# Matrix products emitted in steps of four row tiles or two column tiles beside the chains of two recurrent layers

## The chip, the cores and the metric

The kernel runs on one core of a Trainium2 chip. The metric is the device time of one execution in microseconds (us), lower is better. Five engines work side by side, each on its own queue of instructions and each in the order of its queue: TensorE (PE in the profile, its weight loads PEld), VectorE (DVE), ScalarE (ACT), GpSimd (POOL) and SyncE (SP, which issues most of the DMAs).

## The reference, cut to what matters

The model is one attention block with expert retrieval, followed by two layers of a recurrent network of width 1024 over 528 positions (16 learned tokens and 512 of the input). Only the two recurrent mixers are touched by the change:

```python
def gated_deltanet(h, w_in, w_conv, a_log, dt_bias, w_norm, w_out):
    qkv, z, beta_pre, a_pre = jnp.split(h @ w_in, ...)
    qkv = causal_conv_silu(qkv, w_conv)
    ...
    o = chunk_gated_delta_rule(q, k, v, g, beta)   # a triangular solve and a scan over chunks
    o = rms_norm(o, w_norm) * jax.nn.silu(z)
    return o @ w_out

def mlstm(h, w_in, gate_bias, w_norm, w_out):
    q, k, v, o, gates = jnp.split(h @ w_in, ...)
    ...                                            # a scan over chunks
    return (rms-normed scan output * sigmoid(o)) @ w_out
```

Each mixer is thus a large product in (`h @ w_in`), a recurrence over chunks of positions that is a long chain of small dependent products, and a large product out.

## The kernel before, in words

All tensors lie with the features on the 128 partitions and the positions along the free axis; a large product takes one tile of 128 output features at a time ("column tile") and runs over the 8 tiles of 128 input features ("row tiles"). To keep float32 accuracy each operand is split in a high and a low part, so one row tile is three matmuls for each half of the 528 positions: six matmuls of 264 columns (lines 71, 72 and 76 in `mm_segs`). A column tile of the products in is 8 row tiles, so 48 matmuls; a column tile of the product out of one pair of heads is 2 row tiles, so 12 matmuls. Both accumulate in one of two PSUM tiles of two banks each (`Acc`); VectorE empties them (lines 1544 and 1558 for the products in, line 1605 for the product out).

The gated delta net (`gdn_block`) works on eight pairs of heads, q = 0 to 7, one pass for each. Two chains run over the passes. The preparing chain (`prepare`, then `tokens`) builds the inverse of each chunk's triangular matrix: norms (line 1633), the products `kk` and `kq` (1673, 1674), a long VectorE stretch that ends in `ex` (1691), the product `rep` (1697), another VectorE stretch, and then three levels, each of transposes `xt` (1734), products `py` (1740) and products `pz` (1752). `tokens` turns k and v (1769, 1777). The scanning chain (`scan`) runs over six chunks: the state times k and q (`pks` 1798, `pqs` 1803), VectorE's `rr` (1801), `pv` (1810), ScalarE's `vr` (1812), `psu` and `po` (1817, 1831), VectorE's new state `S` (1823) and output `ot` (1836), which is then normed on ScalarE and GpSimd (1839 to 1843). A third one (`normed`) turns the finished outputs (`ofm`, 1863) and splits them into `oh` and `ol` (1866, 1868), on which the product out works.

What stands where in the program is set by a planner, `Weave.run`: the chains and the stream of large products (`products2`) are Python generators. A chain yields the TensorE time of what it has just emitted and the time after which its next piece is due; whenever a chain is due it is emitted, and otherwise the stream of products is advanced to its next `yield`, which says what that step cost. `gemm_steps` yields after every two row tiles (12 matmuls, 1.3 us in the planner's account), `out_part` after every column tile (12 matmuls, 1.35 us). The planner's clock is a plan and not a measured time. A unit of products may be emitted once its `ready` test holds: q and k of a pass when the scan two passes back is done, v when the tokens of the pass before are turned, z and the product out when `normed` has delivered. In all, the products in of this layer are 48 column tiles and the products out 64.

The compiler of the kernel language then takes the emitted order as a priority and places an instruction that is emitted later ahead of one that it expects to be still waiting. The order on TensorE's queue is fixed after that.

`mlstm_block` does the same for four pairs of heads, with `interleave` in the place of the planner: it advances the products or the chain (`core`), whichever has done the smaller share of its total. Its products in go through `gemm_steps` as well (23 column tiles); its product out (`unit_out`) has a loop of its own.

Of the kernel before, what the change touches and what calls it, by code (L numbers as in the profile page):

```python
# [17 lines left out]

P = 128
D = 1024  # L20
KT = 8
S = 512
NM = 16
# [41 lines left out]
def mm_segs(nc, x, items, start, stop):  # L65

    xh, xl = x
    for s in range(len(items[0][0])):
        sl = items[0][0][s][1]
        for segs, (lh, ll) in items:  # L70
            nc.tensor.matmul(segs[s][0], lh, xh[:, sl], start=start, stop=False)  # L71
            nc.tensor.matmul(segs[s][0], ll, xh[:, sl], start=False, stop=False)  # L72
    for s in range(len(items[0][0])):
        sl = items[0][0][s][1]
        for segs, (lh, _) in items:
            nc.tensor.matmul(segs[s][0], lh, xl[:, sl], start=False, stop=stop)  # L76


def setup(tc, es, A):
# [27 lines left out]
    g.queue = []  # L107
    g.h = [None] * KT
    h_tiles(g)
# [3 lines left out]
def h_tiles(g):  # L113
    for k in range(KT):
        g.h[k] = g.res.tile([P, T], F32, tag=f"h{k}", name=f"h{k}")
# [44 lines left out]
def wpre(g, name, *idx):  # L160

    key = (name, idx)
    if key not in g.pre:
        wstart(g, name, *idx)
        g.pre[key] = wload(g, g.raw.pop(key), g.wp, 3)


def wget(g, name, *idx):

    key = (name, *idx)  # L170
    wpre(g, *key)
    if key in g.queue[:1]:
        g.queue.pop(0)
        for k in g.queue[:2]:
            wpre(g, *k)
        for k in g.queue[2:3 if g.third is None else 4]:
            wstart(g, *k)
    return g.pre.pop((name, idx))


def gemm_fm(g, segs, name, ct, rhs):


    run_steps(gemm_steps(g, segs, name, ct, rhs, lambda: None))
# [66 lines left out]
def rsqrt_rows(g, segs, n):  # L251

    rs = g.np_.tile([P, T], F32, tag="rs", name="rs", bufs=1)
    for p, sl in segs:
        g.nc.scalar.activation(rs[:, sl], p, AF.Sqrt, bias=g.eps, scale=1.0 / D)
    g.nc.vector.reciprocal(rs[:, 0:n], rs[:, 0:n])
# [46 lines left out]
def xn_tiles(g):  # L303
    xh = [g.res.tile([P, T], F32R, tag=f"xh{k}", name=f"xh{k}") for k in range(KT)]
    xl = [g.res.tile([P, T], F32R, tag=f"xl{k}", name=f"xl{k}") for k in range(KT)]
    return xh, xl
# [152 lines left out]
def gemm_steps(g, segs, name, ct, rhs, out):  # L459

    npc, _, nk, _ = g.A[name][ct].shape
    for pc in range(npc):
        hi, lo = wget(g, name, ct, pc)
        for k in range(nk):
            mm_segs(g.nc, rhs(pc * nk + k), [(segs, (hi[:, k], lo[:, k]))], pc == 0 and k == 0, pc == npc - 1 and k == nk - 1)
            if k % 2:
                yield 1.3
    out()


# [107 lines left out]
def attention_block(g, tail):  # L578

    tc, nc, A = g.tc, g.nc, g.A  # L580
    with ExitStack() as es:
# [12 lines left out]
        ni = NormIn(g, "norm1", NM, S, lambda tag: sp.tile([P, 512], F32, tag="sb", name=tag, bufs=6) if tag == "xt" else gp.tile([P, 512], F32, tag="gate0", name=tag))  # L594
        for k in range(KT):
            nc.sync.dma_start(g.h[k][:, NM:], A["xT"][k])
            if k < 2:
                wpre(g, "w_in", 0, k)
        for k in range(KT):
            ni.step(k)  # L600
# [364 lines left out]
class Rows:  # L965


    def __init__(self, g, es):
        self.g = g
        nc = g.nc  # L970
        self.p = es.enter_context(g.tc.tile_pool(name="p_rows", bufs=1))
        self.x = self.p.tile([P, D], F32, name="rx")
        self.o = self.p.tile([P, D], F32, name="ro")
        self.hid = self.p.tile([P, NJ], F32, name="rhid")
# [38 lines left out]
    def step(self):  # L1013

        nc = self.g.nc
        while self.nf < min(self.n + UG, 2 * NJ):
            e, j = divmod(self.nf, NJ)
            t = self.p.tile([P, D], F32, tag="row", name="row", bufs=UG)
            nc.gpsimd.indirect_dma_start(out=t, out_offset=None, in_=(self.U, self.V)[e],  # L1019
# [371 lines left out]
def v2(t):  # L1391
    return t.rearrange("p (s n) -> p s n", s=2)
# [5 lines left out]
class GdnNorm:  # L1398
# [30 lines left out]
    def rows(self, ps, ms1):  # L1429
# [6 lines left out]
        nc.gpsimd.memset(ms1[:, 0:NM], 1.0)  # L1436
        nc.vector.tensor_scalar(ms1[:, NM:], p1, 1.0 / D, EPS, op0=ALU.mult, op1=ALU.add)
        rs = self.g.np_.tile([P, T], F32, tag="rs", name="rs", bufs=1)
        for p, sl in zip(p2, SEG2):
            nc.vector.scalar_tensor_tensor(rs[:, sl], ms1[:, sl], EPS * D, p, op0=ALU.mult, op1=ALU.add)  # L1440
        nc.scalar.activation(rs, rs, AF.Sqrt, scale=1.0 / D)
# [18 lines left out]
def gdn_block(g, ni, tail):  # L1460
    tc, nc, A = g.tc, g.nc, g.A
    with ExitStack() as es:
# [72 lines left out]
        def fm(ct, out):  # L1535
            segs, ps = acc.get()
            return gemm_steps(g, segs, "gdn_in", ct, ni.X, lambda: out(ps))
# [60 lines left out]
        def out_part(q, c4):  # L1598
            hi, lo = wget(g, "gdn_out", q, c4)
            for i in range(4):  # L1600
                ct = 4 * c4 + i
                segs, ps = acc.get()
                for k in range(2):
                    mm_segs(nc, done["og", q][k], [(segs, (hi[:, 2 * i + k], lo[:, 2 * i + k]))], k == 0, k == 1)
                nc.vector.tensor_tensor(v2(g.h[ct]), v2(g.h[ct]), ps, op=ALU.add)
                if q == 7:
                    tail.step(ct)
                yield 1.35
            clk.put(("out", q, c4))

        def units_out(q):
            return [([("gdn_out", q, c4)], lambda: clk.ready(("og", q)), lambda c4=c4: out_part(q, c4)) for c4 in range(2)]
# [358 lines left out]
def mlstm_block(g, ni, tail):  # L1971

    tc, nc, A = g.tc, g.nc, g.A
    with ExitStack() as es:
# [70 lines left out]
        def unit(ct, ready, out, n=T):  # L2045
            def fn():
                segs, ps = acc.get(n)
                if n == S:
                    segs = [(ps, slice(NM, T))]
                return gemm_steps(g, segs, "mlstm_in", ct, ni.X, lambda: out(ps))  # L2050
            return [("mlstm_in", ct, 0)], ready, fn
# [224 lines left out]
```

## Time and profile before

| | |
|---|---|
| median of 3 timed runs | 3642.78 us (3641.7 to 3643.01) |
| the profiled execution, its own time | 3628.02 us |
| its span, first to last instruction | 3626.3 us |
| TensorE busy | 3483.1 us, 96% of the span |
| gated delta net, about 1940 to 2640 us | TensorE busy 675.08 of 700 us, granted clock 0.95 |
| mLSTM, about 3015 to 3265 us | TensorE busy 237.97 of 250 us, granted clock 0.99 |

The profile is of one execution. A matmul's record shows how long it was in the array, and records overlap; the pitch from one start to the next tells the rate. One float32 matmul of the chains shows as two records. "Idle before" is the time in which the engine did nothing just before an instruction, and the arrow names what ended it.

### The profile page before, as it was taken

What the parts mean: (1) busy time and instruction counts of PE and PEld (TensorE: products, weight loads), DVE (VectorE), ACT (ScalarE), POOL (GpSimd) and SP (SyncE); (2) the same over time, 40 slices, a digit from 0 to 9 for tenths busy, and PEclk for the clock granted to TensorE, in tenths of its full rate; (3) what the DMA queues carried; (4) which work ended last, traced back from release to release, by engine and by line L of the source; (5) the groups of instructions that cost most, each with busy time, mean ns of one, the idle gap of its engine ahead of it and who ended that gap; (6) DMA issues with size and microseconds to landing.
All of it is one profiled execution on the core that took longest, in us unless ns stands there. A gap on an engine that the chain in (4) does not pass through costs nothing. (4 is left out here: it accounts for less than half of the span.)

```text
span 3626.3 us, 56462 instructions
## 1 busy us (share of the span) xinstructions
PE 3483.1 (96%) x21979; PEld 3164.9 (87%) x21979; DVE 2399.4 (66%) x4395; ACT 1591.4 (44%) x2998; POOL 776.2 (21%) x828
## 2 busy tenths in 40 slices
PE   8999999999898889999999999999999999999999
PEld 6777888898887779999998899999899998878887
DVE  5764457999967658888887677767643345564433
ACT  4555333333477763333346444445422235343222
POOL 2421010333322232333332322222100003120000
PEclk9999999999999999999998999999999999999999
DMA  4233233566678889999972121111132322213222
GB/s 134 76 88 88 82 124 122 198 225 221 233 237 279 270 299 369 358 360 353 363 257 77 56 63 57 47 52 52 48 98 90 94 88 83 75 59 99 93 93 93
DMA packets 169492, 557.60 MB, mean 154 GB/s; under 512 B 19617, under 2 KB 20130, under 8 KB 169224
## 3 DMA queue, kind: packets, MB, share of 16 engines
q1 hardware_dynamic: 90228, 313.50, 26.1%
q0 software_dynamic: 49136, 170.64, 14.2%
q10 hardware_dynamic: 29860, 69.84, 5.3%
q8 instruction: 173, 2.83, 0.3%
q14 instruction: 95, 0.78, 0.1%
HBM read 492.20 MB, written 55.41 MB: 151 GB/s over the span
## 5 line engine op out<-in xcount | busy, mean ns | idle before, releaser
L72 PE MATMUL ps<-xh,wlo 128*128 128x264 f32 (+2 forms) x3296 | 1051.3, 331 | 45.0 <-DVE wlo L149 44.8
L71 PE MATMUL ps<-xh,whi 128*128 128x264 f32 (+2 forms) x3296 | 1069.6, 337 | 18.8 <-ACT xh L288 13.5
L149 DVE TENSOR_TENSOR wlo<-raw,whi 128x1024 fp32r<-128x1024 f32 x562 | 718.6, 1279 | 531.2 <-ACT whi L147 524.8
L147 ACT ACTIVATE whi<-raw 128x1024 fp32r<-128x1024 f32 x562 | 594.5, 1058 | 978.9 <-PE ps L76 782.6
L76 PE MATMUL ps<-xl,whi 128*128 128x264 f32 (+2 forms) x3296 | 813.1, 331 | 6.5 <-DVE xl L289 6.4
L72 PEld LDWEIGHTS ps<-xh,wlo 128*128 128x128 f32 x3296 | 629.6, 192 | 91.5 <-DVE wlo L149 61.4
L71 PEld LDWEIGHTS ps<-xh,whi 128*128 128x128 f32 x3296 | 630.2, 192 | 59.3 <-ACT xh L288 15.9
L76 PEld LDWEIGHTS ps<-xl,whi 128*128 128x128 f32 x3296 | 563.6, 192 | 39.3 <-DVE xl L289 8.9
L1019 POOL DMA_INDIRECT row<-in_peer_ur_dram,rix x128 | 146.1, 1142 | 465.7 <-DVE row L1028 372.1
L71 PE MATMUL ps<-ah,whi 128*128 128x264 f32 (+1 forms) x768 | 230.1, 320 | 0.0
L72 PE MATMUL ps<-ah,wlo 128*128 128x264 f32 (+1 forms) x768 | 229.9, 320 | 0.0
L55 PE MATMUL ps<-ah,whi 128*128 128x384 f32 x640 | 215.5, 337 | 0.0
L56 PE MATMUL ps<-ah,wlo 128*128 128x384 f32 x640 | 215.1, 336 | 0.0
L1019 POOL DMA_INDIRECT row<-in_peer_v_dram,rix x128 | 138.1, 1079 | 276.9 <-DVE ro L1032 261.5
L280 POOL TENSOR_TENSOR ssum<-ssum,sq 128x512 f32<-128x512 f32 (+1 forms) x49 | 75.1, 1538 | 460.4 <-ACT sq L279 459.8
L1028 DVE SCALAR_TENSOR_TENSOR row<-row,rx 128x1024 f32<-128x1024 f32 x128 | 164.0, 1283 | 6.2 <-DMA row<-in_peer_ur_dram,rix 6.2
L1333 ACT ACTIVATE ah<-gt 128x384 fp32r<-128x384 f32 x128 | 67.3, 526 | 227.4 <-DVE gt L1331 227.4
L76 PE MATMUL ps<-al,whi 128*128 128x264 f32 (+1 forms) x768 | 163.2, 321 | 0.0
L1214 ACT ACTIVATE hot<-hot,lt 128x128 f32<-128x128 f32 x384 | 122.0, 390 | 93.3 <-DVE hot L1212 89.6
L1032 DVE SCALAR_TENSOR_TENSOR ro<-row,rhid,ro 128x1024 f32<-128x1024 f32 x127 | 162.4, 1278 | 0.6 <-DMA row<-in_peer_v_dram,rix 0.4
L71 PEld LDWEIGHTS ps<-ah,whi 128*128 128x128 f32 x768 | 144.3, 188 | 11.4
L72 PEld LDWEIGHTS ps<-ah,wlo 128*128 128x128 f32 x768 | 144.3, 188 | 10.9
(429 smaller groups left out, 6184.7 us busy)
## 6 DMA issues: line engine op xcount, KB each, us to landing
raw<-in_peer_u_dram SPq DMA_DIRECT2D x128, 512.0 KB, 5.5
raw<-in_peer_v_dram SPq DMA_DIRECT2D x128, 512.0 KB, 6.9
raw<-in_ff_up_dram SPq DMA_DIRECT2D x64, 512.0 KB, 3.4
raw<-in_ff_down_dram SPq DMA_DIRECT2D x64, 512.0 KB, 3.5
at<-Ad POOLq DMA_DIRECT2D x32, 768.0 KB, 7.2
raw<-in_gdn_in_dram SPq DMA_DIRECT2D x48, 512.0 KB, 3.5
Gd<-G ACTq DMA_DIRECT2D x62, 384.0 KB, 3.2
gt<-Gd ACTq DMA_DIRECT2D x62, 384.0 KB, 5.2
```

Of the source, the lines that this page charges most:

```text
L55: nc.tensor.matmul(out, lh, rh, start=start, stop=False)
L56: nc.tensor.matmul(out, ll, rh, start=False, stop=False)
L71: nc.tensor.matmul(segs[s][0], lh, xh[:, sl], start=start, stop=False)
L72: nc.tensor.matmul(segs[s][0], ll, xh[:, sl], start=False, stop=False)
L76: nc.tensor.matmul(segs[s][0], lh, xl[:, sl], start=False, stop=stop)
L147: nc.scalar.activation(hi, raw, AF.Copy)
L149: nc.vector.tensor_tensor(lo, raw, r32(hi), op=ALU.subtract)
L280: g.nc.gpsimd.tensor_tensor(self.t[:, 0:n], self.t[:, 0:n], sq[:, 0:n], op=ALU.add)
L1019: nc.gpsimd.indirect_dma_start(out=t, out_offset=None, in_=(self.U, self.V)[e], in_offset=bass.IndirectOffsetOnAxis(ap=self.ix[:, j:j + 1] ...
L1028: o = nc.vector.scalar_tensor_tensor(t, t, 1.0, self.x, op0=ALU.mult, op1=ALU.mult, accum_out=a)
L1032: o = nc.vector.scalar_tensor_tensor(self.o, t, a, self.o, op0=ALU.mult, op1=ALU.add)
L1214: nc.scalar.activation(oh[:, j], o2[:, j], AF.Copy, scale=lt[:, 2, 4 * t4 + j:4 * t4 + j + 1])
```

## The change

`gemm_steps` yields after every four row tiles (24 matmuls) instead of two, with 2.6 us for the step instead of 1.3; `out_part` yields after every second column tile, with 2.7 us instead of 1.35 for one. What is computed, the number of instructions, the tiles and the buffers stay the same.

```diff
+STEP = 4
@@ gemm_steps
             mm_segs(g.nc, rhs(pc * nk + k), [(segs, (hi[:, k], lo[:, k]))], pc == 0 and k == 0, pc == npc - 1 and k == nk - 1)
-            if k % 2:
-                yield 1.3
+            if k % STEP == STEP - 1:
+                yield 0.65 * STEP
@@ out_part
                 if q == 7:
                     tail.step(ct)
-                yield 1.35
+                if i % 2:
+                    yield 2.7
             clk.put(("out", q, c4))
```

## Rows read from the trace of the kernel before

**Rows 1.** The page: span, and each engine's busy time, share and instructions.
```profile
span 3626.3 us, 56462 instructions
PE 3483.1 (96%) x21979; PEld 3164.9 (87%) x21979; DVE 2399.4 (66%) x4395; ACT 1591.4 (44%) x2998; POOL 776.2 (21%) x828
```

**Rows 2.** Busy time by stretch: both layers, and the last scan.
```profile
core 0: us, PE busy (x) PEld busy (x) DVE busy (x) ACT busy (x) POOL busy (x), PEclk, DMA share, GB/s
1940.00:2640.00 700.00, 675.08 (x5849) 639.84 (x5848) 505.26 (x1222) 343.31 (x798) 178.77 (x226) 0.95 0.19 58
3015.00:3265.00 250.00, 237.97 (x1596) 200.94 (x1595) 152.54 (x306) 120.86 (x304) 51.51 (x73) 0.99 0.22 72
2573.60:2605.60 32.00, 31.99 (x255) 31.18 (x256) 16.10 (x33) 15.05 (x48) 5.32 (x12) 1.00 0.20 65
```

**Rows 3.** Waits of TensorE, 1940 to 2640 us: total us, times, longest.
```profile
PE rep L1697 <- DVE ex L1691: 10.0, 8, 2.9
PE ps L71 <- DVE h L1605: 4.9, 4, 1.6
```

**Rows 4.** Timeline of TensorE: start, us, instruction xcount, idle before: rep of two passes.
```profile
2204.30 1.72 PE L1697 MATMUL rep<-ex,nblk 88*88 88x450 f32 x4 [0.82 <-DVE ex L1691]
2279.34 0.96 PE L1697 MATMUL rep<-ex,nblk 88*88 88x450 f32 x2 [0.82 <-DVE ex L1691]
```

**Rows 5.** The same view, a step of products between two scan pieces, q = 7.
```profile
2582.88 0.60 PE L1831 MATMUL po<-vr,dt 88*88 88x128 f32 x4
2583.24 0.37 PE L71 MATMUL ps<-oh,whi 128*128 128x264 f32 x1
2583.44 0.28 PE L72 MATMUL ps<-oh,wlo 128*128 128x264 f32 x1
2583.57 0.28 PE L71 MATMUL ps<-oh,whi 128*128 128x264 f32 x1
```

**Rows 6.** The same view: first products beside that scan, its last piece, and ofm.
```profile
2570.09 0.47 PE L71 MATMUL ps<-oh,whi 128*128 128x264 f32 x1
...
2602.21 0.60 PE L1831 MATMUL po<-vr,dt 88*88 88x128 f32 x4
...
2605.57 1.07 PE L1863 MATMUL ofm<-c_ident,ot 88*128 88x88 f32 x12
```

**Rows 7.** Timelines of TensorE, DVE and ACT: the scan's links in its last chunks.
```profile
2595.58 0.61 PE L1817 MATMUL psu<-vr,kd 88*128 88x128 f32 x4
2596.23 0.61 DVE L1823 SCALAR_TENSOR_TENSOR S<-S,lastb,psu 128x128 f32<-128x128 f32 x2 [3.65 <-PE psu L1817]
2598.78 0.60 DVE L1801 SCALAR_TENSOR_TENSOR rr<-pks,na,vs 88x128 f32<-88x128 f32 x2
2600.28 0.60 PE L1810 MATMUL pv<-rr,Z 88*88 88x128 f32 x4
2600.92 0.38 ACT L1812 ACTIVATE vr<-pv 88x256 f32<-88x256 f32 x1
2605.35 0.69 ACT L1843 ACTIVATE ot<-ot,ss 88x128 f32<-88x128 f32 x2 [1.08 <-POOL ss L1841]
```

**Rows 8.** Busy time in a level stretch, and TensorE's timeline there.
```profile
2226.73:2236.97 10.24, 10.24 (x84) 9.49 (x83) 4.23 (x10) 5.71 (x12) 7.01 (x7) 0.50 0.17 41
2226.37 0.41 PE L1734 MATMUL xt<-c_ident,Z 44*44 44x44 f32 x6
2226.71 0.59 PE L71 MATMUL ps<-xh,whi 128*128 128x264 f32 x1
...
2234.97 0.42 PE L71 MATMUL ps<-xh,whi 128*128 128x264 f32 x1
2235.19 0.42 PE L72 MATMUL ps<-xh,wlo 128*128 128x264 f32 x1
```

**Rows 9.** Waits of TensorE in the mLSTM layer, 3010 to 3270 us.
```profile
PE inter L2170 <- ACT nd L2171: 2.9, 2, 1.7
```

## The prediction

> **What bounds the kernel now.** I read the page first. TensorE is busy 96% of the span and no other engine over 66% [rows 1], so a reordering can gain only what TensorE loses in the two layers that it touches. The busy times by stretch give that loss: in the gated delta net TensorE is busy 675.08 of 700 us, so 24.9 us are idle; in the mLSTM 237.97 of 250, so 12.0 us are idle [rows 2]. The change alters no instruction and no count, so the rest of its effect can only come from where TensorE's instructions stand: idle time, the price of going from a chain's piece to a product and back, and the granted clock, 0.95 in the first layer against 0.99 in the second [rows 2].
>
> The list of waits says which idle time there is: the first entry is `rep`, which waits 10.0 us in eight passes for VectorE's `ex` [rows 3], most passes 0.82 us [rows 4]; the next, 4.9 us, is the last product out waiting for its PSUM tiles [rows 3], after all chains have ended, where the emission has no freedom and the change none either. The passes follow each other at 2279.34 - 2204.30 = 75.0 us [rows 4], with almost no other idle time: TensorE's work sets the period, the chains do not.
>
> The timeline then shows how the steps lie. Beside the last scan they lie as emitted: a piece of the scan, twelve products, the next piece [rows 5]; this begins at 2570.09 and ends with the last piece at 2602.21 [rows 6], and over these 32 us TensorE is busy 31.99 us [rows 2]. In the level stretch it is otherwise: single products, cut out of their step, stand between the transposes [rows 8]. So the emitted order is kept where everything is ready, and where a chain is late the compiler fills the hole with whatever product is free, whatever the step size.
>
> **The change, part by part.**
>
> (a) *Fewer crossings.* The first product after a scan piece takes 2583.44 - 2583.24 = 0.20 us to the next start, the following ones about 0.12 (2583.57 - 2583.44 = 0.13) [rows 5]: a crossing costs 0.08 us. The gated delta net has 48 x 4 + 64 = 256 steps before and 128 after, so at most 128 x 0.08 = 10.2 us are saved, and nothing where the compiler mixes the two streams anyway [rows 8]. Both patterns are in the trace; I take half, -5.1. In the mLSTM 23 x 4 = 92 steps become 46: at most 3.7, taken -1.8.
>
> (b) *`rep` later in the queue.* Between the last `kq` and `rep` the planner now puts products in pieces of 2.6 instead of 1.3, so `rep` stands about one short step later, and VectorE has more time for `ex`. That is more than the 0.82 us that are missing [rows 4], if the step really lies there; where the products have run out by then, nothing changes. Bounds 0 and 8 x 0.8 = 6.4 us; I take about half, -3.
>
> (c) *The pool of the last pass.* While the scan of q = 7 runs, there are only 8 column tiles of the product out and 2 of z left, 8 + 2 x 4 = 16 short steps. Today they cover the 15 links of chunks 1 to 5 one for one (the last gets two). Now they are 8 long steps, each of which stands behind one link: they are used up after `pv` of the third chunk, and what follows has no cover. The links bare: `vr` ends at 2600.92 + 0.38 = 2601.30, 0.42 us after `pv` (2600.28 + 0.60); `S` ends at 2596.84, 0.65 us after `psu` (2595.58 + 0.61), of which `po`, which follows `psu`, covers 0.4; `rr` takes 0.60 us, of which `pqs` covers 0.4 [rows 7]. Together 0.42 + 0.25 + 0.2 = 0.87 us a chunk, and two chunks 1.7. After the last `po`, which ends at 2602.81 [rows 6], `ot` is normed until 2605.35 + 0.69 = 2606.04 [rows 7]: 3.2 us, covered now by the last two steps, then bare. Sum 4.9 us; up to 1.4 comes back, since ScalarE has the eviction of z out of the way earlier. I take +4.
>
> (d) *Levels and tokens of the last pass.* The same happens once before: v of q = 7 and z of q = 6 are 16 short steps beside twelve pieces of `prepare` and `tokens`; as 8 long ones they run out during the levels. I count four to six bare pieces at 0.42 to 0.87 us: 2 to 5, taken +3; below, 0, if scan pieces of q = 6 fall there.
>
> (e) *The clock.* In a level stretch of the steady passes TensorE is busy all of 10.24 us and its clock is 0.50 (1.2 of 2.4 GHz); before the fall it did transposes and small products with single large products between them, before the rise a run of large products [rows 8]. A product then takes 2235.19 - 2234.97 = 0.22 us, against 0.12 [rows 5, 8]. Some 24 products in such a stretch lose 24 x 0.10 = 2.4 us, and the transposes about 1: 3.5 us, an estimate. Bare pieces, as in (c) and (d), look more like that stretch than like the rest; none to two further stretches, 0 to 7 us, taken +2.
>
> (f) *mLSTM core.* With half as many steps, a core piece more often follows a core piece; the longest such wait today is 1.7 us and all are 2.9 [rows 9]. Products of the next pair are free to fill in. 0 to 6, taken +2.
>
> (g) *Chains behind longer steps.* VectorE's additions and evictions keep their number; a chain's piece stands on average 0.5 x 12 x 0.12 = 0.7 us later on TensorE's queue. In passes 1 to 6 I cost this at nothing: TensorE's other work hides it, as the period is work and not chain [rows 4]. If that cover is gone, it is the slower rival below.
>
> The sum: -5.1 - 1.8 - 3 + 4 + 3 + 2 + 2 = +1.1 us on the profiled execution's 3628.02, so 3629.1; that execution is 14.8 us under the median of the timed runs, and with the same distance the median goes from 3642.78 to about 3644.
>
> **The rivals.**
>
> *The covers run out in every pass (slower).* The products of a pass are gated: q and k of the next pass wait for a scan to end, v for the tokens. Long steps use up what is open early in a pass, behind links that need 0.2 to 0.9 us [rows 7], and the later links and the levels stand bare. Then each of six passes pays two or three chunks at 0.87 plus one more half-clock stretch of 3.5 us, as in (c) and (e): 2.5 to 6 us, together 15 to 36, less the 10 of (a) and (b), plus the 11 of (c) to (f): 3659 to 3680. It decides once more than about 1 us per pass can't be filled. For it: the product-poor level stretch exists today [rows 8]. Against it: the fill-in seen there, and PSUM has room for two column tiles (96 products, about 11.7 us) to be drawn forward.
>
> *The gains in full (faster).* (a) and (b) at their ends, -10.2 - 3.7 - 6.4, with only (c) to pay: -16, 3627. For it: the regular alternation of [rows 5], where each crossing would be saved. Against it: the broken steps of [rows 8].
>
> *The clock stays up (faster).* Runs of products twice as long could keep the clock at its upper level through the levels. The mean of 0.95 over 700 us [rows 2] is about 700 x 0.05 / 0.5 = 70 us at 0.50, as much as seven stretches of 10.24 us; at 3.5 us each, -24, so 3619. Against it: what stands between the levels today is single products that the compiler placed, and a step's size does not change what is ready there.
> The Trainium skill speaks for this rival: "TensorE: Matmul & The Clock Gate", section "Loop structure matters more than you think", says that the loop structure decides whether matmuls stay warm, and asks for matmuls kept back to back. The trace agrees that the long runs have the full clock, but shows the clock low in a stretch in which TensorE is never idle [rows 8].
>
> *The change hardly reaches the queue (no change).* Emission is a priority only; if the compiler's placing evens it out, the time is 3643 within 3 us. For it: [rows 8]. Against it: [rows 5, 6], where the steps lie as emitted.
>
> **How the numbers follow.** My forecast, gains and losses about even, has 0.32 and lies between 3636 and 3652; no change at all 0.13; the covers run out in every pass 0.30; the gains in full 0.16; the clock stays up 0.09. Bounds 0.2% either way (7.3 us, about what a measurement of this kernel can tell from no change): 3635.5 to 3650.1. The two middle cases lie inside, 0.45 with nearly all of their range; slower is the first rival, 0.30; faster the two others, 0.25. The predicted time is the forecast's, 3644. The range for 8 in 10 goes from 3626, just past the gains in full, to 3668, the middle of the slower rival; about 0.09 is left out below and 0.1 above.
>
> **What would show it.** After the change: steps of 24 beside the last scan, eight of them, then pieces of the scan with no product between them from the third chunk's `psu` on, and TensorE idle for some 3 us before `ofm`. The entry of `rep` among the waits falls from 10.0 towards 4, or (b) is wrong. The distance from `rep` to `rep` in the steady passes stays at 75.0 us or falls by about 1; if it grows by 2 or more, the slower rival holds, and the idle time or the half-clock stretches in that pass say which half of it. The busy-time rows of the mLSTM stay within 3 us. The forecast is wrong if the gated delta net's stretch changes by more than 7 us either way.

## The result and the profile after

The change makes the kernel slower: the median goes from 3642.78 us (7 runs in this comparison, 3629.42 to 3646.69) to 3658.5 us (7 runs, 3654.81 to 3670.54), a ratio of 1.0053 (95% interval [1.0033, 1.0073]). The same kernel run again in another set (`e7_change_again` below) gave 3658.33 us and again 1.0053 [1.0034, 1.0073]. The forecast was 3644, about even, and is 14.5 us short. The time lies above the 3650.1 up to which the prediction spoke of no change, so the sign is that of the first rival. The range of 3626 to 3668 held it because it reached to the middle of that rival, not because the sum was right.

One thing has to be known before the traces are compared. The profiled execution of after took 3670.54 us and is the longest of its seven, that of before took 3628.02 us and is shorter than any of its seven here, so the spans below differ by 42.5 us where the medians differ by some 16. The second run's profiled execution (3651.04 us, span 3649.2 us) has the same order and is used beside it. It is the shortest of its ten, as that of before is shorter than its seven, so these two compare better: their spans differ by 22.9 us.

The page of after: span, and TensorE's busy time, share and instructions ([rows 1] of before).

```profile
span 3668.8 us, 56447 instructions
PE 3511.0 (96%) x21979; PEld 3189.5 (87%) x21979; DVE 2393.3 (65%) x4395; ACT 1602.7 (44%) x3003; POOL 770.7 (21%) x828
```

Busy time by stretch in after: the gated delta net, the mLSTM (35 us later than in before), the two parts of a level stretch of the fourth pass, q = 3 (columns as in [rows 2]).

```profile
1940.00:2640.00 700.00, 666.78 (x5635) 630.22 (x5633) 470.24 (x1186) 338.53 (x781) 165.23 (x219) 0.92 0.18 55
3050.00:3300.00 250.00, 236.60 (x1567) 199.93 (x1567) 143.99 (x297) 118.55 (x297) 46.39 (x70) 0.96 0.22 70
...
2228.50:2231.40 2.90, 0.41 (x5) 0.25 (x3) 1.33 (x2) 0.98 (x4) 1.94 (x2) 1.00 0.28 34
2231.40:2262.00 30.60, 30.56 (x229) 28.52 (x230) 11.12 (x27) 11.56 (x33) 7.71 (x9) 0.56 0.14 45
```

In the first layer TensorE now is idle 33.2 of 700 us, against 24.9 in [rows 2], and its clock is 0.92 instead of 0.95. In the mLSTM 13.4 us are idle instead of 12.0. The list of waits names what is new. TensorE in after, 1900 to 2700 us: total us, times, longest ([rows 3]).

```profile
PE rep L1700 <- DVE ex L1694: 7.8, 8, 2.3
PE xt L1737 <- ACT xe L1738: 6.2, 3, 2.5
...
PE psu L1820 <- ACT vr L1815: 4.2, 5, 2.3
PE ps L73 <- DVE h L1607: 3.3, 2, 2.2
PE ps L73 <- DVE xs L1546: 2.3, 2, 1.7
...
PE ofm L1866 <- ACT ot L1846: 1.8, 1, 1.8
```

`rep` has fallen from 10.0 to 7.8 us, as step (b) wanted. But an entry that was not there stands second: a transpose of the levels, `xt`, waits 6.2 us for ScalarE's copy `xe`, twice for 2.5 us and once for 1.1. It is to be found in the two passes that were steady before. In the timeline `rep` of these passes now stands as follows ([rows 4]; the next one begins at 2386.69).

```profile
2215.89 1.75 PE L1700 MATMUL rep<-ex,nblk 88*88 88x450 f32 x4 [0.59 <-DVE ex L1694]
...
2301.30 1.75 PE L1700 MATMUL rep<-ex,nblk 88*88 88x450 f32 x4 [0.57 <-DVE ex L1694]
```

The distance has grown from 75.0 to 85.4 us, twice. So "the period is work and not chain" no longer holds there. The pass ahead of these two, as long in before (75.0 us), has become shorter. All three hold 288 products each in both kernels, so their lengths can be compared. In the second run, `rep` from this pass on:

```profile
2138.92 1.72 PE L1700 MATMUL rep<-ex,nblk 88*88 88x450 f32 x4 [0.72 <-DVE ex L1694]
2209.35 1.75 PE L1700 MATMUL rep<-ex,nblk 88*88 88x450 f32 x4 [0.58 <-DVE ex L1694]
2288.29 1.75 PE L1700 MATMUL rep<-ex,nblk 88*88 88x450 f32 x4 [0.58 <-DVE ex L1694]
2367.86 1.75 PE L1700 MATMUL rep<-ex,nblk 88*88 88x450 f32 x4 [0.58 <-DVE ex L1694]
```

These are 70.4, 78.9 and 79.6 us, together 228.9 against 225.0 in before (242.7 in the first profile, of which the first pass has 71.9).

The three queues at the first of the waits of `xt` show what happens. TensorE in after:

```profile
2228.53 0.39 PE L1737 MATMUL xt<-c_ident,Z 88*77 88x88 f32 x3
2231.44 0.72 PE L1737 MATMUL xt<-c_ident,Z 88*77 88x88 f32 x3 [2.53 <-ACT xe L1738]
```

ScalarE, GpSimd and VectorE in after, at the same place:

```profile
2226.93 0.62 ACT L1809 ACTIVATE oi<-pqs,rqe 88x128 f32<-88x128 f32 x2
2230.42 0.69 ACT L1846 ACTIVATE ot<-ot,ss 88x128 f32<-88x128 f32 x2 [2.87 <-POOL ss L1844]
2231.02 0.64 ACT L1738 ACTIVATE xe<-xt 77x264 f32<-77x264 f32 x2
2231.56 0.37 ACT L1815 ACTIVATE vr<-pv 88x256 f32<-88x256 f32 x1
...
2227.89 2.50 POOL L1844 TENSOR_TENSOR ss<-ss,powers 88x2 f32<-88x2 f32 x1
...
2227.93 0.76 DVE L1550 SCALAR_TENSOR_TENSOR y<-xs,c_vecs,y 128x528 f32<-128x528 f32 x1
2228.61 1.22 DVE L151 TENSOR_TENSOR wlo<-raw,whi 128x1024 fp32r<-128x1024 f32 x1
```

Read it upwards from TensorE. The transpose needs its PSUM tile emptied by `xe` on ScalarE. `xe` stands in ScalarE's queue behind the scaling of a scan output (`ot`, line 1846), work that nobody needs soon. The scaling waits 2.87 us for `ss`, the inverse root that GpSimd takes of two numbers per partition. And this small operation takes 2.50 us: it ends at 2230.39, 0.56 us after VectorE has done a step of the convolution (`y`) and split a tile of weights (`wlo`). `vr`, a link of the scan, is held up behind it as well. In before the same three pieces stand in another order. ScalarE and GpSimd of before, the level stretch of the same pass:

```profile
2213.32 0.66 ACT L1735 ACTIVATE xe<-xt 77x264 f32<-77x264 f32 x2 [2.94 <-PE xt L1734]
...
2215.00 0.37 ACT L1735 ACTIVATE xe<-xt 77x264 f32<-77x264 f32 x1
2217.10 0.70 ACT L1843 ACTIVATE ot<-ot,ss 88x128 f32<-88x128 f32 x2 [1.73 <-POOL ss L1841]
...
2215.96 1.10 POOL L1841 TENSOR_TENSOR ss<-ss,powers 88x2 f32<-88x2 f32 x1
```

The copies are through before the scaling waits, and `ss` takes 1.10 us. In before none of the 48 `ss` powers of the layer runs while VectorE splits weights; they take 0.7 (37), 0.8 (2) and 1.1 us (9). In after two of the 48 do, and these two take 2.50 us; the same two do in the second run.

Right after the wait the clock falls: from 2231.43 on it is 0.50 for 13.65 us, 1.00 for 3.41 and 0.50 again for 13.65, where before had one stretch of 10.24 us [rows 8]. TensorE was busy 0.41 of the 2.90 us ahead of it (third row of the stretches above). But a fall in this stretch is not new: in before the clock falls there too, at 2226.73, with no such wait ahead of it [rows 8]. The second run shows what belongs to the order and what to one execution: it has the same waits of 2.53 us, but 10.2 and 17.1 us at 0.50 in these two passes instead of 30.7 and 30.7. In the whole layer its idle time is 39.0 us and its time at 0.50 is 75.1 (after 37.8 and 119.5, before 24.9 and 64.9; counted from 1940 us to the first eviction of the next block). In its list of waits an entry of the same family stands third. TensorE in the second run, 1940 to 2680 us:

```profile
PE xt L1737 <- ACT xe L1738: 6.2, 3, 2.5
PE ps L78 <- POOL ol L1871: 4.5, 3, 3.9
```

The 3.9 us, its longest single wait, are in the second pass: a product waits for `ol`, which stands in GpSimd's queue behind four operations of 4.6 us together (`at` and `dt`, the first of which waits 1.64 us for a DMA). In after the same entry is 1.3 us in all.

### The profile page after: what moved, and what is told of

Its sections match the earlier page's. It is cut to its first block, busy times and chain, and to the rows that moved or that the text cites. A ratio compares the mean times of both kernels' runs of the same rounds, so it can differ in the third digit from the quotient of the medians.

```text
span 3668.8 us, 56447 instructions
## 1 busy us (share of the span) xinstructions
PE 3511.0 (96%) x21979; PEld 3189.5 (87%) x21979; DVE 2393.3 (65%) x4395; ACT 1602.7 (44%) x3003; POOL 770.7 (21%) x828
## 4 chain that ended last, share of the span: by engine, by line
PE 70%; DVE 15%; ACT 7%; issue 4%; POOL 2%; DMA 2%; ACTq 0%; SPq 0%; DVEq 0%; POOLq 0%
PE ps L73 14%; PE ps L74 14%; PE ps L78 14%; PE ps L57 4%; PE ps L60 4%; PE ps L58 4%; DVE wlo L151 3%; DVE row L1030 2%; ACT hot L1216 2%; PE acc L57 2%; PE acc L58 2%; PE acc L60 2%; ACT ab L1237 2%; ACT whi L149 1%; PE pz L1755 1%
## 5 line engine op out<-in xcount | busy, mean ns | idle before, releaser
L151 DVE TENSOR_TENSOR wlo<-raw,whi 128x1024 fp32r<-128x1024 f32 x562 | 710.7, 1265 | 528.5 <-ACT whi L149 516.5
L73 PEld LDWEIGHTS ps<-ah,whi 128*128 128x128 f32 x768 | 144.3, 188 | 11.3
```

Source lines behind the costliest of these rows:

```text
L151: nc.vector.tensor_tensor(lo, raw, r32(hi), op=ALU.subtract)
```

## The experiments

All were timed beside the kernel before in three sets, each set on one chip; the medians of before were 3640.65, 3641.42 and 3641.42 us. The time of one program moves with the clock: over the 35 executions of before in the first set it rises by 0.38 us for each microsecond at 0.50 (the time at 0.50 is taken as twice what the mean granted clock lacks of 1, times the span); in the other two sets it is 0.45 and 0.39, so prices by 0.38 below are rough. Where that matters, the clock stands beside the result.

**The change once more**, as a second profile and as the neighbour of the second set:

> The changed kernel as it is, beside the next three on one chip. Its first profile has 119.5 us at half clock in the gated delta net and 37.8 us idle; with the mLSTM's steps short, the same layer showed 71.7 and 42.4. If the clock's share in that first profile was chance: half clock 70 to 100 us now, the layer's stretch 10 to 20 us shorter than in the first profile, and the time 12 to 20 us over the kernel before. If the order itself holds the clock down: about 119 us again.

Measured: 3658.33 us (10 executions), 1.0053 [1.0034, 1.0073]; its waits and distances stand above. With 75.1 us at 0.50 in the first layer it falls in the range of the first case: much of the first profile's 119.5 us was that one execution.

**One of the two loops alone.** `p1_products_in_only` keeps the long steps of `gemm_steps` and gives `out_part` its old ones; `p2_products_out_only` the reverse.

```diff
 p1, against the change
-                if i % 2:
-                    yield 2.7
+                yield 1.35
 p2, against the change
-            if k % STEP == STEP - 1:
-                yield 0.65 * STEP
+            if k % 2:
+                yield 1.3
```

> The products in take steps of four row tiles as in the change, the product out keeps steps of one column tile. Theory A (a pass's products are spent too early, wherever the long steps stand): 192 of the 256 steps of the gated delta net are of this kind, so most of the loss stays, 9 to 16 us over the kernel before, and in the last pass the 8 column tiles of the product out cover eight links again, so the time from the last rep to the first eviction of the feed-forward falls from 126 to about 120 us. Theory B (the pairs of column tiles do the harm, since two evictions stand one behind the other on VectorE): 0 to 5 us over the kernel before.

> The product out alone takes steps of two column tiles. Theory A: 64 of 256 steps, in the last pass half of the pool: 2 to 6 us over the kernel before, tail (last rep to first eviction of the feed-forward) 118 to 122 us against 116.5. Theory B: 10 to 16 us over.

Measured: 3645.7 us, 1.0008 [0.9992, 1.0024], and 3639.02 us, 0.9992 [0.9978, 1.0006]. Neither half can be told from before, though both together cost 17 us, and neither theory has both times right. If the 17 us were spread evenly over the long steps of the gated delta net, p1 with 192 of 256 would be 12.7 us over before, and its interval ends at 8.7. Yet p1 is not without loss: its trace has 35.4 us of idle time in the first layer against 24.9, while its executions had some 7 us less at 0.50 than those of before (mean clock 0.9781 against 0.9771). The trace of p1 has the same collision once, in the same pass (distance 81.4 us), with another victim: the squares `sq`, for the norms. ScalarE, GpSimd and TensorE of p1:

```profile
2261.15 0.69 ACT L1845 ACTIVATE ot<-ot,ss 88x128 f32<-88x128 f32 x2 [2.91 <-POOL ss L1843]
2261.75 0.60 ACT L1808 ACTIVATE oi<-pqs,rqe 88x128 f32<-88x128 f32 x2
2262.25 0.63 ACT L1629 ACTIVATE sq<-k 128x528 f32<-128x528 f32 x1
...
2257.93 3.19 POOL L1843 TENSOR_TENSOR ss<-ss,powers 88x2 f32<-88x2 f32 x1
...
2262.94 1.34 PE L1635 MATMUL pn<-ones,sq 128*88 128x1 f32 x8 [2.90 <-ACT sq L1629]
```

In p2 no `ss` power of the layer takes over 1.4 us, and the distances of these passes are 76.2 and 76.1 us.

**Short steps where the prediction saw the pool run out.** `p3_last_pass_short` is the change with the old steps for the column tiles beside the last pass and its scan (v of q = 7, z of q = 6 and 7, product out of q = 6).

```diff
+SHORT = (30, 31, 44, 45, 46, 47)
-            return gemm_steps(g, segs, "gdn_in", ct, ni.X, lambda: out(ps))
+            return gemm_steps(g, segs, "gdn_in", ct, ni.X, lambda: out(ps), 2 if ct in SHORT else STEP)
-                if i % 2:
+                if q == 6:
+                    yield 1.35
+                elif i % 2:
                     yield 2.7
```

> The changed kernel, but with short steps for what stands beside the last preparation and the last scan (v of pass 7, z of passes 6 and 7, product out of pass 6). If the tail's loss is the spent pool: the tail falls from 126.1 to 116 to 118 us, and the time by 8 to 10 us, to 6 to 10 us over the kernel before. If the tail is long because the clock or the earlier passes make it so: within 3 us of the changed kernel.

Measured: 3652.5 us, 1.0037 [1.002, 1.0054], 6 us off the change. From the last `rep` to the first eviction of the next block it takes 120.2 us, against 116.5 in before, 126.1 in after and 127.1 in the second run; TensorE's idle time there is 8.3 us, against 8.1, 11.3 and 10.7. So short steps at the end of the layer give back about 6 us. In the traces 2.4 to 3.0 of it are idle time, as steps (c) and (d) have it; the rest goes with the clock, which is at 0.50 for 10.2 us there against 20.5 and 23.9. Some 12 us over before remain.

**The mLSTM.** `p4_mlstm_short` is the change with the old steps in the mLSTM, `e11_mlstm_long_only` is before with the new ones there and nowhere else (a parameter of `gemm_steps`: 2 or `STEP`).

```diff
 p4, against the change
-                return gemm_steps(g, segs, "mlstm_in", ct, ni.X, lambda: out(ps))
+                return gemm_steps(g, segs, "mlstm_in", ct, ni.X, lambda: out(ps), 2)
```

> The changed kernel, but with short steps in the mLSTM. The profiles put 7.2 us of the difference there (247.0 to 254.2 us from the first q eviction to the last addition of the product out). If that is the steps: the time falls by 5 to 8 us, and that stretch returns to 247 us. If it is only the clock's chance in that one execution: within 3 us of the changed kernel.

> Short steps in the gated delta net, long ones in the mLSTM alone. The change with short steps in the mLSTM was 7.5 us faster than the change. If the two layers simply add: 4 to 8 us over the kernel before. If the mLSTM pays only for a clock that the other layer leaves behind: within 2 us.

Measured: 3650.83 us, 1.0033 [1.0018, 1.0048], and 3645.28 us, 1.002 [1.0006, 1.0033]: the kernels with long steps there are some 4 to 7.5 us slower, and by 0.38 the clock alone would account for that (mean clock of p4 0.9774 against 0.9745 for the change, of e11 0.9752 against 0.9774 for before). From the first eviction of q to the last addition of the product out, e11 takes 252.2 us against 247.7 in before; its idle time is 12.4 us against 12.0, and 17.1 us are at 0.50 against 3.4. But p4, with the old steps, has 252.7 us and 20.5 at 0.50 there, and e11 is also slower in the unchanged first layer of its profile (92.2 us at 0.50 against 64.9). Over all traces here, the eight with long steps in the mLSTM take 250.4 to 254.8 us with 13.7 to 20.5 at 0.50; the five with the old steps take 247.7 to 252.7, four of them with 3.4 to 10.2 at 0.50 and p4 with 20.5; e8, with steps of one row tile, takes 251.9 with 17.1. That long steps themselves bring the clock down in the mLSTM is thus likely, but not shown.

**The scaling off ScalarE.** `e5_norm_on_gpsimd` is the change with the scan output scaled on GpSimd, where `ss` is made, in one operation; `e9_before_norm_gpsimd` is before with the same edit.

```diff
-                for e in range(2):
-                    nc.scalar.activation(ot[:, c, e], ot[:, c, e], AF.Copy, scale=ss[:, c, e:e + 1])
+                nc.gpsimd.tensor_tensor(ot[:, c], ot[:, c], ss[:, c].unsqueeze(2).to_broadcast([C, 2, P]), op=ALU.mult)
```

> The changed kernel, with the scaling of the scan's output by its norm done by GpSimd in one instruction a chunk instead of two on ScalarE. Theory C (the loss in the steady passes is one queue: xt waits for ScalarE's copies xe, which stand behind that scaling, which waits for GpSimd's ss): the entry of xt waiting for xe, 6.2 us in three passes, goes to under 1 us, and the time falls by 4 to 8 us against the change. Theory A (the products have run out and TensorE would be idle whoever is late): the wait reappears under another name and the time stays within 2 us.

> The kernel before with the scaling of the scan's output on GpSimd. If the long steps made the wait behind that scaling (theory C): before had no such wait of 2.5 us (its nearest, pz, is 0.37 us in four passes), so the time is within 5 us of the kernel before. If ScalarE's scaling is a cost with any step size: 15 to 20 us below the kernel before, as it took 21 off the change, and then the step size would still cost what it cost.

Measured: 3637.51 us, 0.9992 [0.9977, 1.0008], against 1.0053 for the change in the same set: 21 us less. On before the edit gives 0.9991 [0.9976, 1.0006]. So the scaling's place on ScalarE costs nothing with short steps that can be told from the noise, and without it the kernel with long steps is level with before. The trace of e5 shows the collision itself still there and its victim gone. GpSimd, ScalarE and TensorE of e5, the fourth pass:

```profile
2223.94 2.50 POOL L1844 TENSOR_TENSOR ss<-ss,powers 88x2 f32<-88x2 f32 x1
2226.52 0.61 POOL L1845 TENSOR_TENSOR ot<-ot,ss 88x256 f32<-88x256 f32 x1
...
2224.05 0.66 ACT L1738 ACTIVATE xe<-xt 77x264 f32<-77x264 f32 x2 [0.42 <-PE xt L1737]
2224.78 0.38 ACT L1815 ACTIVATE vr<-pv 88x256 f32<-88x256 f32 x1
...
2224.58 0.62 PE L1737 MATMUL xt<-c_ident,Z 88*77 88x88 f32 x6
2225.04 1.79 PE L1743 MATMUL py<-Z,at 88*77 88x44 f32 x24
```

The power still takes 2.50 us, but `xe` and `vr` pass it by. The distances of the two passes are 75.3 and 71.3 us (with the pass ahead of them 221.1 us, 7.9 less than in the second run of the change), the end takes 121.4 us, 5.8 less, and the idle time of the layer is 33.0 us (second run 39.0, before 24.9). The mean clock of the timed executions is 0.979 against 0.9745, some 34 us less at 0.50, so at 0.38 about 13 of the 21 us are clock and 8 are order. Why the clock is higher without these waits the runs do not show: in after it falls right behind them, in before it falls in the same stretch without one. A rival is left: e5 also takes 0.7 us a chunk off ScalarE, whatever the scaling waits for, and lets the compiler place everything anew. e9 shows that this is worth nothing with short steps; for long ones the next run was to tell.

**The scaling one link later.** `e12_scaling_later` leaves it on ScalarE, but emits it after the next chunk's `vr`.

```diff
+                if c > 0:
+                    for e in range(2):
+                        nc.scalar.activation(ot[:, c - 1, e], ot[:, c - 1, e], AF.Copy, scale=ss[:, c - 1, e:e + 1])
```

> The changed kernel, with the scaling left on ScalarE but emitted one link later, behind the next chunk's vr: the same instructions on the same engines, only the wait for GpSimd's ss is gone from in front of xe. Theory C: xt waits less than 1 us for xe, and 8 to 20 us come off the change. If what helped before was that ScalarE had 0.7 us a chunk less to do: within 4 us of the change.

Measured: 3665.89 us, 1.0076 [1.0054, 1.0098], no better than the change (its mean clock is lower, 0.9723), and the wait of `xt` is 6.2 us as before the edit. ScalarE of e12:

```profile
2238.83 0.69 ACT L1818 ACTIVATE ot<-ot,ss 88x128 f32<-88x128 f32 x2 [2.87 <-POOL xs L1545]
2239.43 0.64 ACT L1738 ACTIVATE xe<-xt 77x264 f32<-77x264 f32 x2
2239.97 0.37 ACT L1815 ACTIVATE vr<-pv 88x256 f32<-88x256 f32 x1
```

(The releaser named is what follows `ss` on GpSimd; the power itself ends at 2236.30 + 2.50 = 2238.80.) The scaling is emitted after `vr` of line 1815 and still stands ahead of it in the queue, and ahead of `xe`. That the compiler places by its own estimate of when `ss` is ready would explain it; the trace does not show that estimate. The edit did not free `xe`, so it says nothing for or against the mechanism, and the rival of less work on ScalarE stays untested with long steps; it says only that moving this emission by one link is not a way out.

**A third buffer.** In p4 a column tile waits twice, 2.5 us each, for VectorE's eviction `xs`; so `e6_three_acc` is the change with three buffers instead of two for the tiles tagged "acc".

```diff
-                y = wk.tile([P, T], F32, tag="acc", name="y", bufs=2)
+                y = wk.tile([P, T], F32, tag="acc", name="y", bufs=3)
```

> The changed kernel with three buffers instead of two for the convolution's sum, which it shares with the normed output. Theory C2 (the products' wait for xs, 4.9 us in two passes, comes from the convolution's y waiting for that buffer until GpSimd has made ol): that entry vanishes and the time falls by 3 to 6 us. If something else holds VectorE or ScalarE there: it stays, and the time is within 2 us of the change.

Measured: 3667.71 us, 1.0067 [1.0041, 1.0094]. The waits of TensorE in e6, 1940 to 2690 us:

```profile
...
PE xt L1737 <- ACT xe L1738: 6.2, 3, 2.5
PE ps L73 <- DVE h L1607: 5.0, 3, 2.2
```

The entry for `xs` has left the list's head, `xt` has not, and no time comes back. The wait for `xs` was a consequence or cost nothing.

**Shorter steps still.** `e8_one_row_tile` has steps of one row tile (`STEP = 1`) in both layers and the old ones in `out_part`.

> Steps of one row tile (6 products) for the products in; the product out keeps steps of one column tile. Crossings: up to 192 more in the gated delta net and 92 in the mLSTM at 0.08 us, 5 to 15 us if each step is a run of its own. If finer steps keep chains earlier and that is what counts: idle time falls by 3 to 6 us and pays for part of it. Forecast 0 to 10 us over the kernel before; below it by more than 4 us speaks for the chains' lateness as the cause of the change's loss.

Measured: 3651.93 us, 1.0036 [1.0021, 1.0052]. Busy time of e8's first layer (columns as in [rows 2]):

```profile
1940.00:2640.00 700.00, 673.20 (x5728) 632.52 (x5727) 488.25 (x1212) 343.02 (x794) 177.75 (x224) 0.94 0.18 56
```

The idle time is 26.8 us, not below before's 24.9. It has no collision (no `ss` power over 1.1 us) and 269 runs of products against 241 in before. Its mean clock is 0.9747 against before's 0.9769: 16 us more at 0.50, so at 0.38 some 6 of its 10.5 us. So finer steps fill no more holes: of the three sizes tried, two row tiles is the best. Why the clock is lower with one is not shown.

**All the remedies together.** `e10_all_three` joins e5, p3 and p4, so that long steps stay only in the passes of the first layer up to the last.

> The change with all its losses met: scaling on GpSimd, short steps beside the last pass and in the mLSTM. The first alone was 3 us under the kernel before; the last pass is worth 4 to 8, the mLSTM 5 to 7, if they add. Forecast 6 to 14 us under the kernel before; more than the kernel before would mean that the pieces do not add.

Measured: 3637.26 us, 0.9986 [0.9971, 1.0]: the fastest ratio of all, but less than was expected, and not surely faster than before. Its idle time in the first layer is 30.7 us, still above 24.9: the first two passes keep 12.2 us (before 7.6). One by one the three remedies took 21, 6 and 7.5 us off the change, 34 in all, where the change costs 17: they give back the same time, for the most part time at 0.50 by the prices above. So the loss cannot be divided among the places by what each remedy is worth.

## Why the prediction was right or wrong

The sign was wrong, and the step that failed is **(g)**: "in passes 1 to 6 I cost this at nothing: TensorE's other work hides it, as the period is work and not chain". The cover was looked for on TensorE alone. What broke it, by the traces, is a chance meeting on the other three engines: the new order puts VectorE's split of weights beside GpSimd's power, ScalarE's scaling waits for the power, and the copy that TensorE needs waits behind the scaling. [Rows 8] showed the copies' stretch but not the queue of ScalarE; the scaling's wait for `ss` was even in [rows 7] (1.08 us before `ot`), read there as a cost of the end only. In the second run the two passes of 75.0 us take 78.9 and 79.6, 8.5 us more, and carry 8.8 us of idle time instead of 2.9; the pass ahead of them takes 70.4, so over the three 4.0 us are left. With the waits gone, in e5, the three take 7.9 us less. The prediction's own criterion, 2 us or more from `rep` to `rep`, is met in two of the three, and its last one too: the layer ends 17.9 us later, where more than 7 was to mean that the forecast is wrong. That (g) failed is shown by the waits and by e5; that it is the whole of the loss is not, since some 13 of the 21 us that e5 gives back are clock.

**The first rival** had the sign, and its 3659 to 3680 begins where the time fell. Its mechanism is only half of it: not every pass pays but two, and what keeps `xt` waiting is not a lack of products but ScalarE's queue, as e5 shows. If the products of a pass had run out, e5 would have stayed slow. Its lower bound does not follow from its own words either: two chunks at 0.87 and a stretch of 3.5 are 5.2 us a pass and not 2.5, which gives some 3675 to 3680, above what was measured.

**(a)** The crossings: 200 runs of products in the layer instead of 241, 64 of them of exactly 24. 41 x 0.08 = 3.3 us saved against 5.1 taken; the pitch at a crossing is 0.205 against 0.122 us, as read in [rows 5]. The mechanism and the price of a crossing hold; 41 crossings went instead of the 64 taken.

**(b)** `rep` waits 7.8 us in after and 7.0 in the second run instead of 10.0: 2.2 to 3.0 us, taken 3. It was to fall "towards 4", and stayed above.

**(c)** The end came as described. TensorE in after, beside the last scan, from the last product on:

```profile
2626.87 0.41 PE L78 MATMUL ps<-xl,whi 128*128 128x264 f32 x2
2627.12 0.61 PE L1820 MATMUL psu<-vr,kd 88*128 88x128 f32 x4
...
2628.68 0.64 PE L1801 MATMUL pks<-S,k 128*88 128x256 f32 x2 [0.52 <-DVE S L1826]
...
2630.38 0.71 PE L1813 MATMUL pv<-rr,Z 88*88 88x128 f32 x4 [0.63 <-DVE rr L1804]
2631.94 0.71 PE L1820 MATMUL psu<-vr,kd 88*128 88x128 f32 x4 [0.85 <-ACT vr L1815]
...
2636.66 0.67 PE L1834 MATMUL po<-vr,dt 88*88 88x128 f32 x4 [1.49 <-ACT vr L1815]
2637.17 1.36 PE L1866 MATMUL ofm<-c_ident,ot 88*128 88x88 f32 x10
```

Steps of 24 up to `psu` of the chunk third from the end, then two chunks bare, as foreseen. The chunk that ends with `psu` at 2631.94 has 0.52 + 0.63 + 0.85 = 2.0 us of idle time, against 0.87 taken; before `ofm` TensorE is idle 1.8 us, where some 3 were foreseen. Over the end as a whole the idle time grows by 3.2 us in after and 2.6 in the second run, against 4 and 3 taken for **(c)** and **(d)**; the length grows by 9.6 and 10.6, though 36 of the 587 products of before's end (some 4 us) now stand ahead of the third `rep`. Most of the rest is the clock (20.5 and 23.9 us at 0.50 against 3.4, about 7 us). p3 gives 6 us back.

**(e)** Further half-clock time was the right kind of loss and too small. The forecast took 2 us; the second run has 10.2 us more at 0.50 in the first layer and 13.7 in the mLSTM, at 0.38 some 9 us, and after had 54.6 and 17.1 more. In the second run's first layer all of it lies in the end, where chain pieces stand bare, as foreseen (23.9 against 3.4 us); the passes ahead of the end have 10.2 us less than in before. In after it lies in the two passes with the waits too.

**(f)** In the mLSTM the idle time grows by 1.2 to 1.4 us (taken 2, less 1.8 for the crossings), and TensorE's busy time in the stretch stays within 3 us (236.60 against 237.97; VectorE's does not, 143.99 against 152.54). The rest of its 5.4 to 7.1 us goes with the clock.

**Sum.** By the second run, its layer ends 17.9 us later: 14.1 us of idle time more, 10.2 us more at 0.50 (some 4 us), less 3.3 for the crossings. About 3 us are left, of which 1.4 were there when the layer began (its first product starts at 1898.71 instead of 1897.35). The term that was mis-sized most is thus idle time: (b), (c) and (d) together took +4 us for this layer, and it came to +14.1. The two passes with the waits have 5.9 us of it, the first two 3.3 (the wait for `ol` among them, which no step had), the end 2.6, the other passes the rest. The rivals *the gains in full* and *the clock stays up* were wrong: the longer runs of products did not keep the clock up. The change reaches the queue, as the steps of 24 show.

## What to carry to other kernels

Where TensorE waits for an engine with an ordered queue, a step of products that is moved is also a step of VectorE's, ScalarE's and GpSimd's work that is moved: before a reordering is costed at nothing, list what stands in ScalarE's queue ahead of each copy that TensorE needs, and what that waits for. Work that nobody needs soon, with a wait on a slower engine in front, can be put on that slower engine, so that it queues behind its own producer; e9 shows that here this costs nothing even where it is not needed. And one loop's effect is no guide to two: p1 and p2 were each level with before, and the gains of three remedies did not add.

## What the runs showed of the hardware

**A small GpSimd operation is held off by large VectorE operations, but only at its start.** The power of 88 x 2 numbers takes 0.69 us by itself. Where a convolution step or a weight split of VectorE begins before it, or at most 0.05 us after, it ends 0.55 to 0.58 us after the last of those that follow each other without a gap: 1.10 us in all behind one step that began 0.21 us ahead of it (before), 2.50 behind a step and a split (0.76 and 1.22 us, after), 3.19 behind a step, a split and a step (p1). The one exception, in e5 and e10 once each, is a power of 2.31 us beside a step, a split and a third step: it ends 0.56 us after the split, and the third step takes 3.06 us instead of 0.76. Where the first of them begins 0.14 us or more after the power, in any trace here, it takes 0.69 to 0.71 us. GpSimd and VectorE in after, in the mLSTM:

```profile
3113.99 0.70 POOL L2185 TENSOR_TENSOR ss<-ss,powers 88x2 f32<-88x2 f32 x1
3114.14 1.23 DVE L151 TENSOR_TENSOR wlo<-raw,whi 128x1024 fp32r<-128x1024 f32 x1 [0.38 <-ACT whi L149]
```

So whether the power costs 0.7 or 2.5 us depends on what VectorE has begun by some 0.1 us after its start.

The Trainium skill, "SBUF — State Buffer", section "SBUF: two separate sides", says that VectorE and GpSimd share a pair of ports, that a VectorE operation with two SBUF inputs excludes a GpSimd operation that reads SBUF, and that the one which starts first keeps the pair for its whole instruction. The traces agree on the exclusion, and on the last point too if a power has the pair only some 0.05 to 0.14 us after the start that the profile shows: at 2227.89 it starts 0.04 us ahead of the convolution step (2227.93) and is held up all the same, at 3113.99 it starts 0.15 us ahead of a split and is not.

**One program, one core, a spread of 25 us.** The 35 executions of before in the first set lie between 3627.31 and 3652.23 us, at mean granted clocks of 0.981 and 0.975. A difference of 17 us between two programs is smaller than that, and only many executions tell it.
